# First block's query path and Exp table load inside the transform stage, its last stores by POOL, row scalings an item later, operand offsets of narrow matmuls

## The chip, the cores and the metric

One core of a Trainium2 chip runs one program. A core has TensorE (PE in the rows of the profile; its weight loads are PEld), VectorE (DVE), ScalarE (ACT), GpSimd (POOL) and SyncE (SP), each with its own queue of instructions that it takes in order, and 16 DMA engines that move data between the device's memory and the on-chip memories. DMAs are issued here by SP and POOL, and wait in the queue of the engine that issues them. The metric is the device time of one execution in microseconds, the median of several runs.

## The reference

One encoder layer for two sequences of 1024 tokens of width 1024, all in float32. A modulated RMSNorm feeds latent attention (4 heads) and a 2-D Fourier transform side by side; both are projected out together, and a SwiGLU feed-forward follows.

```python
h = rmsnorm(x, g_mix) * (1.0 + sc1) + sh1
z = h @ w_in
q_lat, kv_lat, k_pe, f_in = z[..., :o1], z[..., o1:o2], z[..., o2:o3], z[..., o3:]
y_mla = mla_group(q_lat, kv_lat, k_pe, g_q_lat, w_uq, g_kv_lat, w_ukv)
y_four = fourier_group(f_in, w_four)
mix = jnp.concatenate([y_mla, y_four], axis=-1) @ w_out
x = x + ga1 * mix
h2 = rmsnorm(x, g_ffn) * (1.0 + sc2) + sh2
ffn = (jax.nn.silu(h2 @ w_gate) * (h2 @ w_up)) @ w_down
return x + ga2 * ffn
# mla_group, for each query block of a sequence:
#   sc = (q_nope . k_nope + rope(q_pe) . rope(k_pe)) * scale; p = softmax(sc); o = p @ v
# fourier_group: real(fft2(f_in, axes=(sequence, group channel), norm='ortho')) @ w_four
```

The result is normalised once more and returned for both sequences.

## The kernel before

Every matrix product is made of three fp32r matmuls (`mm3`, lines 78 to 80): an operand is split into a high part, cast by ACT (line 62), and a low part, the difference, made by DVE (line 63), and high × high, low × high and high × low add up in one bank of PSUM. PE runs through the stages one after the other:

- **Input projection** (to about 238 us): x is normalised, transposed, and multiplied with the folded input weights; the narrowest products are 448 columns wide (`bank<-wz`).
- **Transform** (238 to 330 us): the DFT of each sequence (`dft`) leaves parts A, B and a Nyquist row `ny`. `fourier_out(s, j)` multiplies them with the folded weights `wm`, `wn`: for each pair (j, g) two banks `pa` (7 matmuls) and `pb` (6), 13 of 512 columns together. ACT copies `pa` to `ea`, DVE makes `ed` = `ea` − `pb` and `ea` + `pb` (lines 135 and 138), and line 735 stores both to `fo_d` in device memory, 256 KB each. `ed` is a ring of three buffers for each sign: a sum can be written when the store of three pairs ago has landed. For j = 0 there are 7 more matmuls (`pn`) for the Nyquist rows. Ahead of the second sequence's eight pairs, `stage3_loads` issues on SP the loads of what attention needs (`ql`, `wqr`, `rc`, `rs`, `lat`, `ckv`) and splits the query weights `wqr` into `wq_h` and `wq_l`.
- **Attention** (330 to about 790 us): 64 items (2 sequences × 4 blocks of 256 rows × 4 heads × 2 halves). For each block the rotary part of the queries is made by `rope_q` (6 matmuls of 256 columns into `gb`; DVE makes three products `qt`, lines 868 to 870, POOL adds them, ACT and DVE split the sum to `qsk`) and turned by `rope_flip` (4 transposes to `pqt`, an ACT copy to `qp`). `absorb_q` makes the rest of a head's queries, `qa` (6 matmuls, then a split). An item's scores are ten matmuls of 512 columns into `ps_s` (lines 904 to 908, two halves), DVE takes the maximum `mx` (913) and `nb` (914), ACT the exponential (916), DVE the reciprocal and the scaling of `p` (917, 918). `flip_p` transposes `p` an item later (930), `values` multiplies with `ckv`. In the first block of each sequence `wv_split` splits the output weights `wv`. Work of earlier blocks is spread over the items: `out_step` gives eight items an output projection, the norm of the new rows (`norm2`: ACT squares, POOL computes `rs_r` in six small steps, DVE scales `xn` at line 824) and the transposes of `xn`.
- **Feed-forward** (from about 799 us): Strassen-like sums on POOL and DVE, and long rows of 512-wide matmuls.

A scheduler orders each engine's queue from the order of the program, its data and its own estimate of when things are ready; `issue_after(x)` lets an instruction into the queue only behind x. A tile's place in on-chip memory follows from the order in which tiles are declared; `tag` and `bufs` make a ring of places that is reused. PSUM has eight banks of 512 columns: eight of one ring `bank` in the transform stage, four for `ps_s`, two for `gb` and two for transposes in attention.

Of the kernel before, what the change touches and what calls it, by code (L numbers as in the profile page):

```python
# [52 lines left out]
def hybrid_encoder_kernel(ctx: ExitStack, tc: tile.TileContext, a: dict):  # L53
# [110 lines left out]
    with ExitStack() as st:  # L164
# [13 lines left out]

        wuqT = w.tile([P, HEADS, QL], F32, tag="hh0", name="wuqT")
        wq = w.tile([P, 2, 768], F32, tag="hl0", name="wq")  # L180
        wz_h = w.tile([P, NC, DZ], F32R, name="wz_h")
# [396 lines left out]
    def load_seq(s, lp=None):  # L578
        lat = [(e if s == 0 else lp).tile([P, 2, N], F32R, tag=f"lat{s}{i}", name=f"lat{s}{i}") for i in range(2)]
        ckv = [e.tile([P, 8, KVL], F32R, tag=f"ckv{i}", name=f"ckv{i}", bufs=1) for i in range(2)]  # L580
        for i in range(2):
            nc.sync.dma_start(rd(lat[i]), lat_d[s][i][:, 2:4, :])
        for i in range(2):
            nc.sync.dma_start(rd(ckv[i]), ckv_d[s][i])
        S[s] = (lat, ckv)
# [6 lines left out]

    def stage3_loads():
        wq_h = e.tile([P, 2, 768], F32R, name="wq_h")
        wq_l = e.tile([P, 2, 768], F32R, name="wq_l")
        load_q(0, 0)
        for c in range(2):
            wqr = half("wqr")
            wqr2 = half("wqr2")
            nc.sync.dma_start(wqr, wq_d[:, c, 0:512])  # L600
            nc.sync.dma_start(wqr2[:, :256], wq_d[:, c, 512:768])
            split(wq_h[:, c, 512:768], wq_l[:, c, 512:768], wqr2[:, :256])
            split(wq_h[:, c, 0:512], wq_l[:, c, 0:512], wqr)
        rc = e.tile([P, 8, ROPE], F32, name="rc")
        nc.sync.dma_start(rc, a["ropec"])
        rs = e.tile([P, 8, ROPE], F32, name="rs")
        nc.sync.dma_start(rs, a["ropes"])
        load_seq(0)
        return wq_h, wq_l, rc, rs

    with ExitStack() as st:
# [11 lines left out]
        nyt = w.tile([P, NT], F32R, name="ny")  # L623
# [24 lines left out]
        def dft(s):  # L648
            z, od = zh.pop(s)
            A = [w.tile([P, 2, NT], F32R, tag=f"A{i}", name=f"A{i}", bufs=1) for i in range(2)]  # L650
            B = [w.tile([P, 2, 512], F32R, tag=f"B{i}", name=f"B{i}", bufs=1) for i in range(2)]
            for q in (0, 2, 1) if s == 0 else (0, 1):
# [12 lines left out]
                if q == 2:  # L665
                    ah = w.tile([NY2, NT], F32R, name="nyh")
                    al = w.tile([NY2, NT], F32, name="nyl")
                else:
                    ah, al = A[0][:, q, :], A[1][:, q, :]
# [41 lines left out]
        def fourier_out(s, ABn, j):  # L711
# [3 lines left out]
            for g in range(2):  # L715
# [11 lines left out]
                add(ed[1], ea, pb, nc.vector)  # L727
                if j == 0:
                    pn = bank2()
                    for q in range(2):  # L730
                        mm3(pn[:2, :], A[0][:, q, 512:514], A[1][:, q, 512:514], wm[0][:, q, gs], wm[1][:, q, gs], q == 0, False)
                    nc.tensor.matmul(pn[:2, :], ny[:, 512:514], wn[:, gs], start=False, stop=True)
                    nc.scalar.copy(ed[1][0:1, :], pn[0:1, :])
                for u in range(2):
                    nc.sync.dma_start(fo_d[s][rows(j, u), gs], ed[u])
# [34 lines left out]
        for s in range(2):  # L770
            for j in (1, 2, 3, 0):
                fourier_out(s, abn, j)
# [4 lines left out]
            if s == 0:  # L777
# [8 lines left out]
                wq_h, wq_l, rc, rs = stage3_loads()  # L786
    P2.close()
# [28 lines left out]
    def norm2(s, b, u, pool):  # L816
# [7 lines left out]
        here["n"] = sq, nc.vector.tensor_scalar(out=xn, in0=x2, scalar1=r[:, 0:1], scalar2=None, op0=ALU.mult).ins  # L824
        S["xn", s, b, u] = xn

# [14 lines left out]
    def out_step(s, b, i):  # L841
# [5 lines left out]
        if i in (1, 3):  # L847
            norm2(s, b, i // 2, tl)
# [3 lines left out]
    with ExitStack() as st:  # L852
# [3 lines left out]

        def rope_q(s, b, u):
            ql = S["q", s, b]
            ti = 2 * b + u
            us = slice(u * P, u * P + P)  # L860
            pq = gbank()
            for c in range(2):
                mm3(pq[:, :256], ql[0][:, c, us], ql[1][:, c, us], wq_h[:, c, 512:], wq_l[:, c, 512:], c == 0, c == 1)
            pv = pq[:, :256].rearrange("p (h r) -> p h r", h=HEADS)
            t1 = half("qt1").rearrange("p (k h r) -> p k h r", k=2, h=HEADS)
            cb = rc[:, ti : ti + 1, :].broadcast_to([P, HEADS, ROPE])
            sb = rs[:, ti : ti + 1, :].broadcast_to([P, HEADS, ROPE])
            nc.vector.tensor_tensor(out=t1[:, 0], in0=pv, in1=cb, op=ALU.mult)
            nc.vector.tensor_tensor(out=t1[:, 1, :, :32], in0=pv[:, :, 32:], in1=sb[:, :, :32], op=ALU.mult)
            nc.vector.tensor_tensor(out=t1[:, 1, :, 32:], in0=pv[:, :, :32], in1=sb[:, :, 32:], op=ALU.mult)  # L870
            here["p"] = nc.gpsimd.tensor_tensor(out=t1[:, 0], in0=t1[:, 0], in1=t1[:, 1], op=ALU.add).ins
            sk = w.tile([P, HEADS, P], F32R, tag="sk", name="qsk", bufs=2)
            nc.scalar.copy(sk[:, :, :64], t1[:, 0])
            nc.vector.tensor_tensor(out=sk[:, :, 64:], in0=t1[:, 0], in1=rd(sk[:, :, :64]), op=ALU.subtract)
            S["sk", s, b, u] = sk

        def rope_flip(s, b, u):
            sk = S.pop(("sk", s, b, u))
            pt = tbank("pqt", F32R)
            for h in range(HEADS):  # L880
                nc.tensor.transpose(pt[:, h, :], sk[:, h, :], identr)
            qp = w.tile([P, HEADS, P], F32R, tag="qp", name="qp", bufs=4)
            nc.scalar.copy(qp, rd(pt))
            S["qp", s, b, u] = qp

        def absorb_q(s, b, h):
            ql = S["q", s, b]
            pq = gbank()
            hs = slice(h * P, h * P + P)
            for c in range(2):  # L890
                mm3(pq[:, :256], wq_h[:, c, hs], wq_l[:, c, hs], ql[0][:, c, :], ql[1][:, c, :], c == 0, c == 1)
            qa = [w.tile([P, 256], F32R, tag=f"qa{i}", name=f"qa{i}", bufs=3) for i in range(2)]
            split(qa[0], qa[1], pq[:, :256])
            S["qa", s, b, h] = qa

        def scores(s, b, h, u):
# [17 lines left out]
            nc.vector.tensor_scalar(out=nb, in0=mx, scalar1=-SCALE, scalar2=None, op0=ALU.mult)  # L914
            p = w.tile([P, N], F32, tag="p", name="p", bufs=3)
            nc.scalar.activation(p, ps, AF.Exp, bias=nb, scale=SCALE, accum_out=sm)
# [27 lines left out]
        for u in range(2):  # L944
            rope_q(0, 0, u)
        absorb_q(0, 0, 0)
        for u in range(2):
            rope_flip(0, 0, u)
# [28 lines left out]
        def wv_split(i):  # L977
            h, g = i % 4, i // 4
            gs = slice(512 * g, 512 * g + 512)
            split(wv[0][:, h, gs], wv[1][:, h, gs], S.pop(("wv", h, g)))  # L980
# [17 lines left out]
        for k in range(nit + 4):  # L998
# [7 lines left out]
            if k < nit:  # L1006
                s, b, h, u = items[k]
                scores(s, b, h, u)
                nxt = items[k + 8 - k % 8] if k + 8 - k % 8 < nit else None
                i = k % 8  # L1010
                if nxt is not None:
                    if i == 0:
                        load_q(*nxt[:2])
                    if i == 3 and nxt[1] == 0:
                        load_seq(nxt[0], w)
                    if i in (3, 4):
                        rope_q(*nxt[:2], i - 3)
                    if i in (5, 6):
                        rope_flip(*nxt[:2], i - 5)
                if u == 1 and k + 1 < nit:  # L1020
                    absorb_q(*items[k + 1][:3])
# [610 lines left out]
```

## Time and profile before

| | us |
|---|---|
| three runs, median (lowest to highest) | 2095.7 (2093.01 to 2097.82) |
| the profiled execution | 2097.92 |
| its span, first to last instruction | 2096.1 |

The granted clock of PE over the span was 0.987. The page gives for each engine the busy time, its share of the span and the number of instructions. A row of the slices cuts the span into 40 parts of 52.4 us, and each digit is a busy share in tenths, for PEclk the granted clock:

```profile
PE   5899998999999999999999999999999999999998
DVE  2657756766676678687777777666855565567675
ACT  2666524455565546233333346453333333336441
POOL 1455202111312314797787720225545444420142
PEclk8999999999999999999999999999999999999999
```

In a row of the timeline stand the start and the duration in us, the engine, the line, the operation, what is written and what is read, and in brackets how long the engine stood idle before it and what ended that. Matmuls follow each other faster than one of them lasts, so their pace is read from starts, not from durations. A row that ends in x and a number stands for so many instructions in a stretch.

### The profile page before, as it was taken

The numbers are of one execution on the slowest core, as the hardware profiler recorded it, in microseconds if no ns is written. First come the engines' busy times: TensorE is split into PE (matmuls) and PEld (weight loads), VectorE is DVE, ScalarE is ACT, GpSimd is POOL, SyncE is SP. The second block draws the span as 40 slices with busy tenths as digits, with TensorE's granted clock in tenths as the row PEclk, the third lists the DMA queues.
The fourth block names the chain that finished last, engine by engine and source line by source line (L and its number), as shares of the span: only waits on it lengthen the run. The fifth ranks groups of instructions, "written<-read, shape, count | busy, mean of one in ns | idle before, by whom it ended". The sixth has DMA issues, their size and how long they took to land. (4 is left out here: it accounts for less than half of the span.)

```text
span 2096.1 us, 28784 instructions
## 1 busy us (share of the span) xinstructions
PE 2013.3 (96%) x10044; PEld 1669.9 (80%) x10044; DVE 1398.5 (67%) x2087; ACT 905.6 (43%) x1763; POOL 827.8 (39%) x1018
## 2 busy tenths in 40 slices
PE   5899998999999999999999999999999999999998
PEld 2788876888888887788888888877788888888876
DVE  2657756766676678687777777666855565567675
ACT  2666524455565546233333346453333333336441
POOL 1455202111312314797787720225545444420142
PEclk8999999999999999999999999999999999999999
DMA  9585766444454345556555578674423232248662
GB/s 367 190 251 196 233 229 221 94 98 100 137 133 130 122 174 206 188 196 209 166 188 190 176 249 271 223 239 153 150 87 115 101 115 102 86 167 282 229 224 98
DMA packets 184255, 371.30 MB, mean 177 GB/s; under 512 B 19053, under 2 KB 58605, under 8 KB 181037
## 3 DMA queue, kind: packets, MB, share of 16 engines
q1 hardware_dynamic: 166252, 314.00, 45.0%
q0 software_dynamic: 17856, 55.45, 8.9%
q8 instruction: 79, 1.29, 0.2%
q14 instruction: 68, 0.55, 0.1%
HBM read 257.38 MB, written 120.39 MB: 180 GB/s over the span
## 5 line engine op out<-in xcount | busy, mean ns | idle before, releaser
L78 PE MATMUL bank<-H,wh 128*128 128x512 f32 x1232 | 483.7, 393 | 10.2 <-ACT val L1312 5.4
L80 PE MATMUL bank<-H,wl 128*128 128x512 f32 x1232 | 482.7, 392 | 1.9 <-DVE wl L63 1.9
L79 PE MATMUL bank<-H,wh 128*128 128x512 f32 x1232 | 482.9, 392 | 0.0
L138 DVE TENSOR_TENSOR val<-bank,val 128x512 f32<-128x512 f32 x244 | 166.8, 689 | 192.6 <-PE bank L80 186.2
L78 PEld LDWEIGHTS bank<-H,wh 128*128 128x128 f32 x1232 | 233.0, 189 | 62.5 <-DVE val L138 6.8
L80 PEld LDWEIGHTS bank<-H,wl 128*128 128x128 f32 x1232 | 233.1, 189 | 51.4 <-DVE wl L63 2.7
L79 PEld LDWEIGHTS bank<-H,wh 128*128 128x128 f32 x1232 | 233.2, 189 | 48.6
L63 DVE TENSOR_TENSOR wl<-draw,wh 128x512 fp32r<-128x512 f32 x286 | 201.1, 736 | 89.4 <-ACT wh L62 87.9
L62 ACT CAST wh<-draw 128x512 fp32r<-128x512 f32 x286 | 169.0, 620 | 159.1 <-PE bank L79 87.0
L79 PE MATMUL bank<-wl,wh 128*128 128x512 f32 x572 | 224.0, 392 | 3.1 <-DVE wl L63 3.1
L78 PE MATMUL bank<-wh 128*128 128x512 f32 x572 | 222.9, 390 | 0.2 <-ACT wh L62 0.2
L80 PE MATMUL bank<-wh,wl 128*128 128x512 f32 x572 | 222.8, 389 | 0.0
L138 POOL TENSOR_TENSOR val<-val 128x512 f32<-128x512 f32 x58 | 82.5, 1429 | 350.6 <-DVE val L1413 186.8
L62 ACT CAST wh<-rgu 128x512 fp32r<-128x512 f32 x172 | 107.0, 623 | 261.1 <-PE bank L79 201.9
L62 ACT CAST wh<-val 128x512 fp32r<-128x512 f32 x133 | 82.2, 621 | 271.7 <-PE bank L79 245.7
L63 DVE TENSOR_TENSOR wl<-val,wh 128x512 fp32r<-128x512 f32 x133 | 128.4, 968 | 73.0 <-ACT wh L62 72.8
L135 POOL TENSOR_TENSOR val<-rgu 128x512 f32<-128x512 f32 x84 | 119.4, 1421 | 121.4 <-DMA rgu<-in_wgu_dram 86.4
L63 DVE TENSOR_TENSOR wl<-rgu,wh 128x512 fp32r<-128x512 f32 x172 | 158.3, 921 | 5.8 <-ACT wh L62 5.6
L79 PEld LDWEIGHTS bank<-wl,wh 128*128 128x128 f32 x572 | 107.4, 188 | 28.9 <-DVE wl L63 7.0
L78 PEld LDWEIGHTS bank<-wh 128*128 128x128 f32 x572 | 107.4, 188 | 23.1 <-ACT wh L62 0.6
L80 PEld LDWEIGHTS bank<-wh,wl 128*128 128x128 f32 x572 | 107.4, 188 | 21.8
L135 POOL TENSOR_TENSOR val<-val 128x512 f32<-128x512 f32 x89 | 119.2, 1358 | 1.3
(332 smaller groups left out, 4068.0 us busy)
## 6 DMA issues: line engine op xcount, KB each, us to landing
rgu<-in_wgu_dram SPq DMA_DIRECT2D x86, 512.0 KB
draw<-s_d SPq DMA_DIRECT2D x143, 256.0 KB
s_d<-val POOLq DMA_DIRECT2D x88, 256.0 KB, 4.0
draw<-t_d SPq DMA_DIRECT2D x88, 256.0 KB
s_d<-val SPq DMA_DIRECT2D x66, 256.0 KB
draw<-in_w_down_dram SPq DMA_DIRECT2D x55, 256.0 KB
wada<-in_w_ada_dram SPq DMA_DIRECT2D x13, 1024.0 KB
xt<-in_x_dram SPq DMA_DIRECT2D x16, 512.0 KB
```

The lines of the kernel that those rows point to most:

```text
L62: here["a"] = nc.scalar.copy(hi, src).ins
L63: here["v"] = nc.vector.tensor_tensor(out=lo, in0=src, in1=rd(hi), op=ALU.subtract).ins
L78: nc.tensor.matmul(out, lh, rh, start=first, stop=False, skip_group_check=cont)
L79: nc.tensor.matmul(out, lh, rl, start=False, stop=False, skip_group_check=cont)
L80: nc.tensor.matmul(out, ll, rh, start=False, stop=last, skip_group_check=cont)
L135: return eng.tensor_tensor(out=out, in0=x, in1=y, op=ALU.subtract).ins
L138: eng.tensor_tensor(out=out, in0=x, in1=y, op=ALU.add)
```

## The change

- **Query path of the first block.** `rope_q`, `rope_flip` and `absorb_q` move out of the attention stage and take their bank as an argument. Both `rope_q` and the first `absorb_q` now run ahead of the last two pairs (j = 0) of the second sequence's `fourier_out`; the two `rope_flip` run inside the first of these pairs.
- **Stores.** The 16 stores of the second sequence's `fourier_out` are issued by POOL, those of the first still by SP.
- **Loads.** `wqr` is loaded 768 wide into the places that `ckv` takes later, one load for each of two rows; the `ckv` loads then wait for the splits.
- **Tables.** A one-element Exp runs on ACT behind the last split of `stage3_loads`, and a one-element Silu behind the last item's exponential.
- **Splits of wv** are issued behind the `nb` and the exponential of an item.
- **Row scalings.** In `out_step`, `norm2` keeps the scaling of `xn` back; it is issued in the next item, behind that item's `nb`.
- **Offsets.** Tiles of 32 bytes a row that hold nothing (`phase_...`) shift the tiles behind them, and rows of 514 floats get places of 528.

PE at the end of the transform stage, before: the last pair's Nyquist matmuls, then the query path (absorb, rope) in attention's own banks.

```order
L79 MATMUL bank<-wm_3307,A_3208 2x512
L80 MATMUL bank<-wm_3306,A_3209 2x512
L732 MATMUL bank<-wn,ny 2x512
L78 MATMUL gb<-wq_h,ql_3380 128x256
L79 MATMUL gb<-wq_l,ql_3380 128x256
L80 MATMUL gb<-wq_h,ql_3381 128x256
```

And now, the end of the query path, and behind it the first of the last two pairs:

```order
L78 MATMUL bank<-ql_3383,wq_h 128x256
L79 MATMUL bank<-ql_3384,wq_h 128x256
L80 MATMUL bank<-ql_3383,wq_l 128x256
L78 MATMUL bank<-wm_3308,A_3210 128x512
L79 MATMUL bank<-wm_3309,A_3210 128x512
```

and the end of that pair, with the transposes of the rotary part:

```order
L79 MATMUL bank<-wm_3309,B_3212 128x512
L80 MATMUL bank<-wm_3308,B_3213 128x512
L617 MATMUL pqt<-identr,qsk 128x128 x8
L78 MATMUL bank<-wm_3308,A_3210 2x512
L79 MATMUL bank<-wm_3309,A_3210 2x512
```

The query path stands ahead of the last two pairs, its transposes between the first of them and its Nyquist matmuls; after the second pair the scores follow at once.

POOL at the same place, before:

```order
L702 MEMSET wnr 128x512 x4
L871 TENSOR_TENSOR qt_3639<-qt_3639 128x256
L871 TENSOR_TENSOR qt_3654<-qt_3654 128x256
L974 TENSOR_TENSOR wvr_3714<-wvr_3714,gah 128x512 x4
L871 TENSOR_TENSOR qt_3845<-qt_3845 128x256
```

and now:

```order
L745 MEMSET wnr 128x512 x4
L781 DMA fo_d_101<-ed 128x512 x12
L608 TENSOR_TENSOR qt_3563<-qt_3563 128x256
L608 TENSOR_TENSOR qt_3578<-qt_3578 128x256
L781 DMA fo_d_101<-ed 128x512 x4
L989 TENSOR_TENSOR wvr_3720<-wvr_3720,gah 128x512 x4
L608 TENSOR_TENSOR qt_3851<-qt_3851 128x256
```

The two rope additions (`qt`) stand behind twelve stores; the last four stores follow them.

DVE where a row scaling (`xn`) of the first sequence meets the next item's maximum (`mx`), before:

```order
L814 TENSOR_TENSOR x_4397<-x_4397,gb 128x512
L824 TENSOR_SCALAR xn<-x_4397,rs_r 128x1024
L913 TENSOR_REDUCE mx<-ps_s 128x1
L63 TENSOR_TENSOR qa_4742<-gb,qa_4741 128x256
L914 TENSOR_SCALAR nb<-mx 128x1
```

and now:

```order
L866 TENSOR_TENSOR x_4403<-x_4403,gb 128x512
L933 TENSOR_REDUCE mx<-ps_s 128x1
L934 TENSOR_SCALAR nb<-mx 128x1
L879 TENSOR_SCALAR xn<-x_4403,rs_r 128x1024
L63 TENSOR_TENSOR qa_4748<-gb,qa_4747 128x256
```

The scaling has gone behind the maximum and `nb`, and still stands ahead of the low half of `qa`.

The diff, cut to its core:

```diff
+        w.tile([P, 8], F32, name="phase_hh")
         wuqT = w.tile([P, HEADS, QL], F32, tag="hh0", name="wuqT")
         wq = w.tile([P, 2, 768], F32, tag="hl0", name="wq")
+        w.tile([P, 8], F32, name="phase_wz")
...
+    def rope_q(s, b, u, bankf):
...
+    def rope_flip(s, b, u, pt):
...
+    def absorb_q(s, b, h, bankf):
...
+        e.tile([P, 8], F32, name="phase_ql")
         load_q(0, 0)
+        e.tile([P, 8], F32, name="phase_hv")
+        hv = [half("hv") for _ in range(2)]
+        rc = e.tile([P, 8, ROPE], F32, name="rc")
+        rs = e.tile([P, 8, ROPE], F32, name="rs")
+        lat = [e.tile([P, 2, N], F32R, tag=f"lat0{i}", name=f"lat0{i}") for i in range(2)]
+        e.tile([P, 8], F32, name="phase_kv")
         for c in range(2):
-            wqr = half("wqr")
-            wqr2 = half("wqr2")
-            nc.sync.dma_start(wqr, wq_d[:, c, 0:512])
-            nc.sync.dma_start(wqr2[:, :256], wq_d[:, c, 512:768])
-            split(wq_h[:, c, 512:768], wq_l[:, c, 512:768], wqr2[:, :256])
-            split(wq_h[:, c, 0:512], wq_l[:, c, 0:512], wqr)
-        rc = e.tile([P, 8, ROPE], F32, name="rc")
+            wqr = e.tile([P, 768], F32, tag=f"ckv{c}", name="wqr", bufs=1)
+            nc.sync.dma_start(wqr, wq_d[:, c])
+            split(wq_h[:, c, 512:768], wq_l[:, c, 512:768], wqr[:, 512:768])
+            split(wq_h[:, c, 0:512], wq_l[:, c, 0:512], wqr[:, 0:512])
+        e.tile([P, 8], F32, name="phase_e")
         nc.sync.dma_start(rc, a["ropec"])
-        rs = e.tile([P, 8, ROPE], F32, name="rs")
         nc.sync.dma_start(rs, a["ropes"])
-        load_seq(0)
+        load_seq(0, lat)
...
-        nyt = w.tile([P, NT], F32R, name="ny")
+        nyt = w.tile([P, 528], F32R, name="ny")[:, :NT]
...
-            A = [w.tile([P, 2, NT], F32R, tag=f"A{i}", name=f"A{i}", bufs=1) for i in range(2)]
+            A = [w.tile([P, 2, 528], F32R, tag=f"A{i}", name=f"A{i}", bufs=1)[:, :, :NT] for i in range(2)]
...
+                if (s, j, g) == (1, 0, 0):
+                    for u in range(2):
+                        rope_flip(0, 0, u, pp.tile([P, 512], F32R, tag="b", name="pqt").rearrange("p (a b) -> p a b", a=4))
...
-                    nc.sync.dma_start(fo_d[s][rows(j, u), gs], ed[u])
+                    (nc.sync if s == 0 else nc.gpsimd).dma_start(fo_d[s][rows(j, u), gs], ed[u])
...
+                if s == 1 and j == 0:
+                    for u in range(2):
+                        rope_q(0, 0, u, bank2)
+                    absorb_q(0, 0, 0, bank2)
...
+                with tc.issue_after(here["a"]):
+                    nc.scalar.activation(tiny.tile([P, 1], F32, name="warm"), cmask[:, 0:1], AF.Exp)
...
-    def norm2(s, b, u, pool):
+    def norm2(s, b, u, pool, later=False):
...
-        here["n"] = sq, nc.vector.tensor_scalar(out=xn, in0=x2, scalar1=r[:, 0:1], scalar2=None, op0=ALU.mult).ins
         S["xn", s, b, u] = xn
+
+        def scale():
+            here["n"] = sq, nc.vector.tensor_scalar(out=xn, in0=x2, scalar1=r[:, 0:1], scalar2=None, op0=ALU.mult).ins
+
+        if later:
+            S["scale"] = scale
+        else:
+            scale()
...
-            norm2(s, b, i // 2, tl)
+            norm2(s, b, i // 2, tl, True)
...
-        for u in range(2):
-            rope_q(0, 0, u)
-        absorb_q(0, 0, 0)
-        for u in range(2):
-            rope_flip(0, 0, u)
...
-            split(wv[0][:, h, gs], wv[1][:, h, gs], S.pop(("wv", h, g)))
+            with tc.issue_after(here["nb"]), tc.issue_after(here["exp"]):
+                split(wv[0][:, h, gs], wv[1][:, h, gs], S.pop(("wv", h, g)))
...
+                if "scale" in S:
+                    with tc.issue_after(here["nb"]):
+                        S.pop("scale")()
+                if k == nit - 1:
+                    with tc.issue_after(here["exp"]):
+                        nc.scalar.activation(tiny.tile([P, 1], F32, name="warm"), cmask[:, 0:1], AF.Silu)
```

87 lines of the change are left out of this document (41 added, 46 removed).

## The prediction

> **What bounds the kernel now.** I read the page's busy shares first, then the slices, then windows around the slices in which TensorE (PE) is not full.
>
> ```profile
> PE 2013.3 (96%) x10044; PEld 1669.9 (80%) x10044; DVE 1398.5 (67%) x2087; ACT 905.6 (43%) x1763; POOL 827.8 (39%) x1018
> ```
>
> PE is busy 96% of 2096.1 us, so the change can only win where PE stands still or runs at a lower clock. The windows (span, then busy time of PE, PEld, DVE, ACT, POOL, then granted clock, DMA share, GB/s) show where that is near the change:
>
> ```profile
> 300.00:320.00 20.00, 20.00 (x91) 16.25 (x90) 10.21 (x27) 5.59 (x11) 0.22 (x1) 1.00 0.57 192
> 320.00:340.00 20.00, 16.76 (x79) 12.23 (x78) 9.37 (x19) 5.62 (x12) 1.46 (x2) 0.91 0.95 320
> 340.00:360.00 20.00, 15.59 (x72) 13.00 (x71) 14.92 (x25) 12.16 (x22) 12.69 (x9) 0.83 0.39 120
> 360.00:380.00 20.00, 19.53 (x132) 17.53 (x133) 17.72 (x37) 11.70 (x24) 2.30 (x3) 1.00 0.40 135
> ```
>
> The transform stage ends at 330 us and attention begins. In those 40 us PE is idle 3.24 + 4.41 = 7.65 us, and the clock is down by 0.09 and 0.17 of 20 us, which is 1.8 + 3.4 = 5.2 us; together 12.9 us, where the windows on both sides lose 0 and 0.5. Some of the low clock may fall into idle time, so 12.9 is what I take for the whole of it, not a floor.
>
> The timeline tells why (start, duration, work, and in brackets the idle time before it and what ended it):
>
> ```profile
> 326.01 0.40 PE L80 MATMUL bank<-wm,A 128*128 128x512 f32 x1
> 328.32 0.40 PE L80 MATMUL bank<-wm,B 128*128 128x512 f32 x1
> 328.32 0.69 DVE L135 TENSOR_TENSOR ed<-ea,bank 128x512 f32<-128x512 f32 x1 [6.96 <-DMA fo_d<-ed]
> ...
> 333.54 0.39 PE L78 MATMUL gb<-wq_h,ql 128*128 128x256 f32 x1 [3.20 <-DVE ed L138]
> ```
>
> First stall: VectorE (DVE) waited 6.96 us for a store of ed to land, then had eight sums in arrears, and PE, which needs the banks that they read, stood 3.2 us. The stores are late because SP issues them behind the attention loads:
>
> ```profile
> 311.04 0.43 SPq L582 DMA_DIRECT2D lat<-lat_d  x1
> 315.88 0.33 SPq L600 DMA_DIRECT2D wqr<-wq_d  x1
> 318.15 16.33 SPq L735 DMA_DIRECT2D fo_d<-ed  x14
> ```
>
> SP stood 4.4 us (311.47 to 315.88) in front of the second wqr load, and only then came 14 stores, over 16.33 us.
>
> ```profile
> 343.71 1.12 DVE L63 TENSOR_TENSOR wv<-wvr,wv 128x512 fp32r<-128x512 f32 x1 [1.30 <-ACT wv L62]
> 344.96 1.53 DVE L63 TENSOR_TENSOR wv<-wvr,wv 128x512 fp32r<-128x512 f32 x1
> 346.42 1.21 DVE L913 TENSOR_REDUCE mx<-ps_s 128x1 f32<-128x1024 f32 x1
> 346.62 1.28 ACT L916 ACT_TABLE_LOAD   x1
> 347.91 1.11 ACT L916 ACTIVATE p<-ps_s,nb 128x1024 f32<-128x1024 f32 x1
> 348.14 0.27 DVE L870 TENSOR_TENSOR qt<-gb,rs 128x128 f32<-128x128 f32 x1
> 348.56 0.55 PE L78 MATMUL gb<-ql,wq_h 128*128 128x256 f32 x1 [3.96 <-DVE qt L870]
> ```
>
> Second stall: the rope products (qt) of the next block free a bank that PE needs, but stand on DVE behind two splits of wv (2.65 us) and the second maximum; ScalarE (ACT) casts wv too, then loads the Exp table, before the first exponential.
>
> **The change part by part.** *Transition.* Three edits aim at these 12.9 us. The 16 stores of the second sequence go to POOL, so SP's loads no longer stand ahead of them. A POOL store is seen elsewhere in this kernel:
>
> ```profile
> L1248 POOL DMA_DIRECT2D s_d<-val x88: 539/557/653, 854.3 to 1883.1; - x88
> DMA to landing us min/median/max: 2.3/4.0/6.1
> ```
>
> It takes 0.56 us of POOL and lands in 4.0 us, 6.1 at most. PE makes a pair of banks in 13 matmuls; the two L80 rows are ten apart, 2.31 us, so 0.231 each and 3.0 us a pair. The ed ring is three deep, so a buffer has about 9 us less the 1.4 us of its two sums; two issues and the landing need 1.1 + 6.1 = 7.2. It holds, and POOL has 1.1 us of work in each 3.0. On POOL the two rope additions stand behind 12 stores; the last of those follows its own sum, which is before the rope products on DVE in any case.
>
> The first block's query path (12 + 6 matmuls of 256 columns) runs ahead of the last two bank pairs. Its long chain was bare:
>
> ```profile
> 334.55 0.42 DVE L868 TENSOR_TENSOR qt<-gb,rc 128x256 f32<-128x256 f32 x1 [1.07 <-PE gb L80]
> ...
> 337.92 0.41 DVE L874 TENSOR_TENSOR qsk<-qt,qsk 128x256 fp32r<-128x256 f32 x1
> ```
>
> From the first product to the second qsk it takes 338.33 − 334.55 = 3.8 us, at the low clock. In its new place PE has 6 matmuls of absorption (0.7 us) and 13 of 512 columns (3.0) before the eight transposes, 3.7 together: at most 0.4 us of waiting. Then 7 + 13 + 7 matmuls (27 × 0.231 = 6.2 us) cover the two qp copies.
>
> The table load (1.28 us) moves between copies of banks on ACT, which is busy 5.59 of 20 us there: no cost. The wv splits (1.12 and 1.53 us on DVE above) now come after an exponential, one an item, so qt and the maxima are no longer behind them. PE starts the first scores just after the last Fourier matmul; the first probabilities need from the end of item 0's scores a maximum (1.2), nb (0.15), exponential (1.1), and, by estimate from xn and nb, reciprocal and scaling (1.1), 3.6 us, plus handovers that I put at 1.0 by the gaps between the rows above: 4.6. PE has until then the scores of item 1 (10 × 0.231 = 2.3), 12 matmuls of 256 columns at half that (1.4) and half of item 2's scores (1.2): 4.9. So it is just even, and I leave 1.0 us of idle time. Without any cover that chain costs what the second stall cost. Transition: 12.9 − 1.0 = **11.9 us gained**; bounds 0 (stalls of the same size) and 12.9.
>
> *Row scalings an item later.* Before the change xn stands on DVE ahead of the maximum of the next item, and waits for the norm's scalar from POOL. The waits of PE between 400 and 790 us hold five such stalls (total, times, longest), and the timeline shows the first:
>
> ```profile
> PE ps_s L906 <- DVE nb L914: 7.4, 5, 2.1
> ```
>
> ```profile
> 437.00 0.76 DVE L824 TENSOR_SCALAR xn<-x,rs_r 128x1024 f32<-128x1024 f32 x1 [3.70 <-ACT ht L837]
> 437.67 1.22 DVE L913 TENSOR_REDUCE mx<-ps_s 128x1 f32<-128x1024 f32 x1
> 438.80 0.41 DVE L63 TENSOR_TENSOR qa<-gb,qa 128x256 fp32r<-128x256 f32 x1
> 439.27 0.50 PE L906 MATMUL ps_s<-lat,qa 128*128 128x512 f32 x1 [1.10 <-DVE nb L914]
> ```
>
> The matmul needs qa's low half, so DVE's order is the whole matter. The scores that mx reads are done here at 435.8 (the last one starts at 435.38), DVE idle:
>
> ```profile
> 435.38 0.39 PE L908 MATMUL ps_s<-lat,qp 128*128 128x512 f32 x1
> 663.27 1.75 DVE L824 TENSOR_SCALAR xn<-x,rs_r 128x1024 f32<-128x1024 f32 x1 [3.68 <-ACT ht L837]
> 666.53 0.50 PE L906 MATMUL ps_s<-lat,qa 128*128 128x512 f32 x1 [2.08 <-DVE nb L914]
> ```
>
> In the new order mx takes 435.8 to 437.0, nb 0.15, xn 437.15 to 437.9, qa to 438.35: PE goes on at 438.4 instead of 439.27, 0.9 us earlier. In the stalls of 2.08, where xn takes 1.75 beside a POOL sum, the same order gives 663.4 + 1.75 + 0.41 = 665.6 against 666.5, again 0.9. Five times 0.9 is **4.5 us gained**; bounds 0 (qa is still behind xn, and waits with it) and 7.4. xn itself is about 0.15 us later (437.15 for 437.00), which nothing behind it feels: its transposes come an item later.
>
> *Address offsets.* The small tiles and rows of 528 shift operands by 32 bytes. In the input projection the loop's blocks alternate between two pairs of offsets, in pairs, and so does the pace (first and last of 24 matmuls):
>
> ```profile
> 85.47 0.36 PE L78 MATMUL bank<-wz_h,hh 128*128 128x448 f32 x1
> 90.07 0.36 PE L80 MATMUL bank<-wz_h,hl 128*128 128x448 f32 x1
> 109.82 0.37 PE L78 MATMUL bank<-wz_h,hh 128*128 128x448 f32 x1
> 114.57 0.36 PE L80 MATMUL bank<-wz_h,hl 128*128 128x448 f32 x1
> ```
>
> 23 steps take 4.60 us where the offsets modulo 64 bytes are 32 and 0, and 4.75 where they are 32 and 32; all are 32 and 0 after the change. Half of the 384 matmuls, at 6.5 ns, would be 1.2 us; this stage also waits for its inputs, so I take 0.6. The 720 values matmuls of 256 columns (x240 for each of three lines) change in the same way:
>
> ```profile
> L78 PE MATMUL gb<-pt,ckv 128*128 128x256 f32 x240 | 69.3, 289 | 0.0
> ```
>
> At half the step (half the bytes moved) this could be 720 × 3 ns = 2.3 us, or nothing, as I see no pair of offsets of it in the trace; I take 0.4. **1.0 us gained**, bounds 0 and 3.5.
>
> *Silu table.* It moves from 812 us to the end of attention:
>
> ```profile
> 812.06 1.28 ACT L1321 ACT_TABLE_LOAD   x1
> 813.15 0.68 DVE L138 TENSOR_TENSOR val<-bank,val 128x512 f32<-128x512 f32 x1
> 813.88 0.50 PE L78 MATMUL bank<-H,wh 128*128 128x512 f32 x1 [1.18 <-DVE val L138]
> ```
>
> PE waits there for DVE's val, not for ACT, so this brings 0; bounds −0.3 and 0.5.
>
> Sum: 11.9 + 4.5 + 1.0 + 0 = 17.4 us. The profiled execution took 2097.9 us (span 2096.1 and 1.8 around it), so 2080.5 on its account; it lies 2.2 us above the median of 2095.7, so **2078.3 us** for a median.
>
> **The rivals.** *The first softmax stays bare (24%).* Scores of two items are all the work that PE has while DVE and ACT make the first probabilities; I found 4.9 us of matmuls against about 4.6. If the chain is 4 us longer, the 340 to 360 window keeps its loss, 4.41 + 3.4 = 7.8 us: 2078.3 + 7.8 − 1.0 = 2085. For it: the rows of 343 to 348 show three engines crowded there. Against it: table load and wv splits are gone from that chain.
> In this trace a stop of 3.2 us is followed by a low clock (0.91), and the one of 2.08 at 666 is not:
>
> ```profile
> 650.00:680.00 30.00, 27.59 (x176) 24.05 (x175) 18.70 (x32) 17.71 (x39) 7.66 (x11) 1.00 0.49 150
> ```
>
> The Trainium skill, TensorE: Matmul & The Clock Gate, section What's actually happening, has the clock halved after an idle window of about 3.4 us; the trace agrees as far as these two stops go, and by that rule a stop that stays shorter costs only itself: at 3.4 us for my 1.0, 2080.7.
>
> *The scalings gain nothing (10%).* qa stays behind xn, and PE waits as before: 2078.3 + 4.5 = 2083.
>
> *POOL's stores become the wait (slower, 8%).* If POOL could not have three or more stores in flight, each 4.0 us to land, 16 take 64 us where PE makes eight pairs in 24; ed would fill after three pairs, rope's additions would come behind the twelfth store, and PE would stop for up to 64 − 24 = 40 us instead of 12.9: 2095.7 + 40 − 12.9 − 5.5 + 5 (low clock) = 2122. It decides from a store pair slower than 3.0 us on, and exceeds the old time from 12.9 + 5.5 = 18.4 us of stops. Against it: the L1248 rows sit 0.56 us each and in pairs, with no wait for a landing. For it: DMA share is 0.95 at 320 to 340, where SP's stores took 16.33 / 14 = 1.17 us each to issue; at that pace POOL needs 2.3 us a pair, still under 3.0.
> The Trainium skill, SBUF — State Buffer, section Summary: rules for kernel authors, speaks against the move: descriptors that GpSimd writes are starved while DVE runs in a faster two-port mode, so use SP's or ACT's hardware queue. If every store waited for one DVE sum of 0.69 us it would take 1.25, 2.5 us a pair, which still fits; no run here shows it.
>
> *Nothing moves that decides (6%).* DMA share is 0.95 in the first window; if the loads fill it as before, POOL's stores land as late as SP's did, the ring is held as before, and of the 5.5 us elsewhere half comes: 2095.7 − 2.7 = 2093.
>
> **How the numbers follow.** My forecast has 52%, the rivals 24, 10, 8 and 6. A measurement of this kernel tells about 0.2% (4.2 us) from no change. The forecast and the first two rivals are faster by more, 0.86; nothing moves: same, 0.06; stores: slower, 0.08. Low end: transition 12.9, scalings 7.4, addresses 3.5, table 0.5, together 24.3 or 2071.4. High end: both smaller rivals together, 2085 + 4.5, about 2090, with 0.14 left above (the last two rivals) and a little below the low end. Range 2071 to 2090.
>
> **What would show it.** Right: DVE no longer waits for fo_d<-ed near 320 to 330; PE busy over 19 of 20 us and clock 1.00 in the two windows of the transition; L906 waits for nb under 1 us each; wz matmuls at 200 ns throughout. Wrong: PE idle before pqt (rope addition late), before the first ppt (softmax bare), or DVE waiting for POOL's stores. An unknown stall elsewhere in attention, from PE reaching work earlier than its loads, would break the sum.

## The result and the profile after

The changed kernel took 2095.3 us (median of 12 runs, 2092.94 to 2099.37), the kernel before 2094.19 us (12 runs, 2090.89 to 2097.82). The ratio is 1.0004 with a 95% interval of 0.9995 to 1.0013: no change. Forecast were 2078.3 us, and a range of 2071 to 2090.

The gain was there, and was given back elsewhere. The windows of the transition in the profile after (span, then busy time of PE, PEld, DVE, ACT, POOL, clock, DMA share, GB/s) show the first part of it:

```profile
300.00:320.00 20.00, 20.00 (x91) 16.32 (x90) 12.13 (x31) 7.76 (x14) 5.51 (x10) 1.00 0.89 327
320.00:340.00 20.00, 20.00 (x109) 15.33 (x108) 11.04 (x25) 6.71 (x13) 9.71 (x12) 1.00 0.75 272
340.00:360.00 20.00, 18.45 (x121) 16.06 (x120) 18.11 (x35) 12.39 (x25) 6.49 (x6) 1.00 0.13 42
```

PE is idle 1.55 us in 320 to 360 where it was 7.65, and the clock stays at 1.00. The timeline after shows the scores following the last Fourier matmul at once, and the first feed-forward matmul:

```profile
331.65 0.39 PE L778 MATMUL bank<-wn,ny 128*2 128x512 f32 x1
331.90 0.47 PE L924 MATMUL ps_s<-lat,qa 128*128 128x512 f32 x1
...
778.84 0.40 PE L78 MATMUL bank<-H,wh 128*128 128x512 f32 x1
```

In the profile before, that matmul stands here:

```profile
798.75 0.39 PE L78 MATMUL bank<-H,wh 128*128 128x512 f32 x1
```

So the changed kernel enters the feed-forward 19.9 us earlier. Then it loses. The same view of one undisturbed stretch of the feed-forward, first before and then after the change:

```profile
900.00:1150.00 250.00, 249.66 (x1100) 206.11 (x1099) 186.49 (x185) 78.27 (x131) 204.68 (x187) 1.00 0.56 188
```

```profile
900.00:1150.00 250.00, 250.00 (x1077) 202.98 (x1076) 178.21 (x180) 76.89 (x129) 199.18 (x181) 1.00 0.53 182
```

PE is busy throughout and at full clock in both, but starts 1077 matmuls in 250 us instead of 1100: one every 232.1 ns instead of every 227.3. A busy share can't show that; the count in brackets does. These are the matmuls of `H` with the up weights (`bank<-H,wh` and `bank<-H,wl`), 3 × 1232 = 3696 of them. Unrounded the step is 4.85 ns longer, and 3696 × 4.85 ns = 17.9 us. The down matmuls, whose two operands both lie in the places of `wh` and `wl`, keep their 227 ns. From the first to the last of the up matmuls of each sequence the traces show 431.3 us before and 438.8 after for the first sequence, 431.0 and 439.9 for the second; these stretches have waits in them too, and grow by 16.4 us together.

What differs for `H`? In the compiled program, its tiles lie 128 bytes higher than before (`H00` at 77408 instead of 77280), while the weights lie where they lay (151520). The diff doesn't name `H`. The 128 bytes are the two one-element warm-up results: their name `warm` is new in the pool of small tiles, which gives every name four places of 32 bytes, and `H` is laid out behind that pool. Before, the two operands were a multiple of 256 bytes apart; after, 128 more.

In the two traces the gain of 19.9 us and the loss of 16.4 leave 3.5 us, and the changed kernel's profiled execution is 3.8 us the shorter of the two (2094.11 us against 2097.92). It is no gain of the medians: the execution before was 3.7 us above its median of 12 runs, the one after 1.2 below, and −3.8 + 3.7 + 1.2 = +1.1, the distance of the medians.

### The profile page after: what moved, and what is told of

Read it like the earlier page. It is cut to its first block, busy times and chain, and to the rows that moved or that the text cites. A ratio compares the mean times of both kernels' runs of the same rounds, so it can differ in the third digit from the quotient of the medians.

```text
span 2092.3 us, 28786 instructions
## 1 busy us (share of the span) xinstructions
PE 2024.3 (97%) x10044; PEld 1665.8 (80%) x10044; DVE 1399.9 (67%) x2087; ACT 902.8 (43%) x1765; POOL 840.1 (40%) x1034
## 5 line engine op out<-in xcount | busy, mean ns | idle before, releaser
L78 PE MATMUL bank<-H,wh 128*128 128x512 f32 x1232 | 487.9, 396 | 11.9 <-DVE val L138 7.5
L138 POOL TENSOR_TENSOR val<-val 128x512 f32<-128x512 f32 x58 | 83.0, 1439 | 365.3 <-DVE val L1435 187.1
L63 DVE TENSOR_TENSOR wl<-val,wh 128x512 fp32r<-128x512 f32 x133 | 143.1, 1078 | 82.2 <-ACT wh L62 82.2
L933 DVE TENSOR_REDUCE mx<-ps_s 128x1 f32<-128x1024 f32 x64 | 78.2, 1222 | 62.1 <-PE ps_s L928 61.5
```

The lines of the kernel that those rows point to most:

```text
L63: here["v"] = nc.vector.tensor_tensor(out=lo, in0=src, in1=rd(hi), op=ALU.subtract).ins
L78: nc.tensor.matmul(out, lh, rh, start=first, stop=False, skip_group_check=cont)
L138: eng.tensor_tensor(out=out, in0=x, in1=y, op=ALU.add)
L933: nc.vector.tensor_reduce(out=mx, in_=ps, axis=AX.X, op=ALU.max)
```

## The experiments

My theory after the result: the place of `H` takes 15 to 18 us, and everything else in the change gains about 19. The rivals: PE is slower in the feed-forward for another reason (it stands less before; DMA or POOL run differently), or the slow pace only hides stalls that come back. Each run is compared with the kernel before on the same chip in the same batch, so two runs of different batches are best compared by their ratios. A (1) behind a time marks a single execution.

| run | median (runs) | before | ratio, 95% interval |
|---|---|---|---|
| e1_no_shift | 2077.33 (5) | 2096.88 | 0.9906, 0.9892 to 0.9919 |
| e2_before_128 | 2114.63 (4) | 2096.88 | 1.0081, 1.0065 to 1.0097 |
| e3_before_256 | 2097.89 (1) | 2096.88 | |
| e4_before_64 | 2100.87 (1) | 2096.88 | |
| e5_before_32 | 2118.72 (1) | 2094.95 | |
| e6_before_160 | 2119.55 (1) | 2094.95 | |
| e7_before_scale | 2085.34 (4) | 2094.90 | 0.9959, 0.9944 to 0.9974 |
| e8_sp_stores | 2080.56 (1) | 2094.90 | |
| e9_no_phase | 2075.95 (4) | 2094.90 | 0.9911, 0.9897 to 0.9924 |
| e10_scores_0 | 2078.27 (5) | 2094.90 | 0.9920, 0.9907 to 0.9933 |
| e11_path_back | 2083.98 (4) | 2096.11 | 0.9940, 0.9923 to 0.9956 |
| e12_wv_free | 2075.83 (4) | 2096.11 | 0.9905, 0.9890 to 0.9920 |

### The 128 bytes taken out

```diff
-                    nc.scalar.activation(tiny.tile([P, 1], F32, name="warm"), cmask[:, 0:1], AF.Exp)
+                    nc.scalar.activation(tiny.tile([P, 1], F32, name="pc"), cmask[:, 0:1], AF.Exp)
...
-                        nc.scalar.activation(tiny.tile([P, 1], F32, name="warm"), cmask[:, 0:1], AF.Silu)
+                        nc.scalar.activation(tiny.tile([P, 1], F32, name="pc"), cmask[:, 0:1], AF.Silu)
```

> The changed kernel with its two one-element warm-up results put into a ring that exists already (pc), so that no new place is taken in the pool of small tiles and the feed-forward's H tiles lie 128 bytes lower, where they lay before the change. Theory (place): the change gained 19.9 us up to the feed-forward and gave back 14.7 us there, because all 3696 matmuls of H with the up weights start every 231 to 232 ns instead of 227 when H is 128 bytes off against the weights. Then H matmuls are at 227 ns again and the time is 2095.3 - 14.7 = 2080.6 us (2077 to 2083). Rival 1 (PE is slower in the feed-forward because it stood less before, or through DMA traffic or POOL's work): still 232 ns, 2095. Rival 2 (the slower pace hides stalls that come back): 227 ns, but 2090 or more.

Measured: 2077.33 us, 19.6 us under the kernel before, 0.9906 (0.9892 to 0.9919). The stretch of the feed-forward in its profile:

```profile
900.00:1150.00 250.00, 249.81 (x1103) 206.52 (x1102) 189.14 (x184) 78.28 (x131) 205.75 (x186) 1.00 0.55 184
```

1103 matmuls, the old pace. The same instructions in the same order are faster by 18 us (by the medians; 20 by the ratios 1.0004 and 0.9906) when four places of 32 bytes go. Both rivals fall.

### The 128 bytes alone, and other distances

Unused tiles at the start of the pool of small tiles, in the kernel before; here four of 32 bytes, and 8, 2, 1 and 5 in the other runs:

```diff
     tiny = ctx.enter_context(tc.tile_pool(name="tiny", bufs=4))
+    tiny.tile([P, 8], F32, name="shift0", bufs=1)
+    tiny.tile([P, 8], F32, name="shift1", bufs=1)
+    tiny.tile([P, 8], F32, name="shift2", bufs=1)
+    tiny.tile([P, 8], F32, name="shift3", bufs=1)
```

> The kernel before, with 128 bytes a partition of unused tiles in the pool of small tiles and nothing else. Theory (place): H matmuls start every 231 to 232 ns, the feed-forward is 15 us longer, 2109 us (2106 to 2112). Rivals (anything that the change does in time: order, stalls, queues): 227 ns and 2094 us.

> The kernel before with 256 unused bytes. If the distance of the two operands counts modulo 256 bytes or less: 227 ns, 2094 us. If it counts modulo 512 or more, or any shift costs: 231 ns or more, 2109 us.

> The kernel before with 64 unused bytes. If only the offset modulo 64 bytes counts, as my prediction had it: 227 ns, 2094 us (but then the 128 bytes of the other kernel would not count either). If the distance modulo 128 or 256 bytes counts: slower than 227 ns, between 2096 and 2115 us.

> The kernel before with 32 unused bytes: the offset modulo 64 bytes of H against the weights becomes 32 to 0, the distance modulo 256 is 32. If the distance modulo 256 sets the pace in steps of 64: 227 to 229 ns. If unequal offsets modulo 64 are faster, as the input projection suggested: 225 ns or less. If they are slower than the 128 bytes of e2: over 233 ns.

> The kernel before with 160 unused bytes, distance 160 modulo 256, offsets modulo 64 unequal. By the distance alone, between 128 (232.6 ns) and 192: 229 to 233 ns, 2105 to 2114 us. By the input projection's 448-wide matmuls, which are fastest at 160 and slowest at 0: 227 ns or less.

The same stretch in the five profiles, in the order 128, 256, 64, 32 and 160 bytes:

```profile
900.00:1150.00 250.00, 250.00 (x1078) 202.67 (x1077) 178.16 (x181) 76.92 (x129) 202.15 (x183) 1.00 0.53 183
```

```profile
900.00:1150.00 250.00, 249.82 (x1103) 206.54 (x1102) 186.26 (x184) 78.10 (x131) 205.38 (x187) 1.00 0.56 190
```

```profile
900.00:1150.00 250.00, 249.82 (x1091) 204.34 (x1090) 186.69 (x182) 77.54 (x130) 203.48 (x186) 1.00 0.55 186
```

```profile
900.00:1150.00 250.00, 250.00 (x1073) 200.81 (x1072) 179.74 (x179) 76.43 (x128) 200.69 (x181) 1.00 0.53 185
```

```profile
900.00:1150.00 250.00, 250.00 (x1068) 200.97 (x1067) 178.38 (x178) 75.73 (x128) 198.69 (x180) 1.00 0.53 183
```

With 128 bytes the kernel before, which has no other part of the change, takes the changed kernel's pace, 250 / 1078 = 231.9 ns, and loses 17.8 us (13.6 to 20.3 by the interval); I had expected 15. The unused tiles move other operands too: half of the 640 score matmuls go from 229 to 233 ns, about 1 us of the loss. With 256 bytes the old pace is back (226.7), so a distance of 256 bytes is as good as none. In between: 64 bytes 229.1 ns, 32 bytes 233.0, 160 bytes 234.1. The guess that unequal offsets modulo 64 bytes might be faster for 512 columns is wrong: 32 and 160 are the two slowest of the five, 24 us slower in their one run each, and 160 is slower than both of my expectations for it.

One rival is left: that the place of `H` counts by itself, and not its distance from the other operand. The traces settle it. In the last 132 matmuls of the program (`bank<-H`) both operands lie in places of `H`, so unused tiles move them together and leave their distance alone. A third of them, first before, then with 160 bytes (the three numbers behind the count are recorded durations in ns, then come the first and the last start):

```profile
L78 PE MATMUL bank<-H x44: 388/389/390, 2056.6 to 2085.9; 128*128 128x512 f32 x44
```

```profile
L78 PE MATMUL bank<-H x44: 387/389/390, 2078.2 to 2107.5; 128*128 128x512 f32 x44
```

Both take 29.3 us for 129 steps, 227 ns a step, while the up matmuls of the same two runs take 227 and 234. So what counts here is the distance.

### The offsets that the change does name

e1 without the empty tiles and with rows of 514 again, so that all matmul operands lie as far apart as before:

```diff
-        w.tile([P, 8], F32, name="phase_hh")
...
-        e.tile([P, 8], F32, name="phase_ql")
...
-            A = [w.tile([P, 2, 528], F32R, tag=f"A{i}", name=f"A{i}", bufs=1)[:, :, :NT] for i in range(2)]
+            A = [w.tile([P, 2, NT], F32R, tag=f"A{i}", name=f"A{i}", bufs=1) for i in range(2)]
```

> The version of e1 without the small unused tiles and the rows of 528, so that all the operands of matmuls lie as far from each other as in the kernel before. Prediction's term: the offsets bring 1.0 us (0 to 3.5), so this is 2078.3. What e1's trace shows (matmuls of 256 columns 1 to 6 ns faster, scores of 512 columns 3 to 4 ns slower, 448 columns the same) makes 1152 x 2 to 3 ns gained against 640 x 3.7 lost: 0 within 1 us, 2077. If the offsets do what the change's words say: 2080 or more.

Measured: 2075.95 us, 0.9911 (0.9897 to 0.9924) against e1's 0.9906: no difference that can be told. The offsets bring nothing as a whole. Their parts can be seen in the starts of the matmuls: with them the 256-column matmuls of `pt` and `ckv` go from a median of 120 ns to 119 (117 in the changed kernel), and the scores, whose `qa` and `qp` have moved away from `lat`, from means of 229 to 233.

The next kernel tries to have both, and brings the scores' operands back to a multiple of 256 bytes:

```diff
-        e.tile([P, 8], F32, name="phase_e")
+        e.tile([P, 56], F32, name="phase_e")
...
-                        load_seq(nxt[0], [w.tile([P, 2, N], F32R, tag=f"lat1{i}", name=f"lat1{i}") for i in range(2)])
+                        load_seq(nxt[0], (w.tile([P, 48], F32, name="phase_lat1"), [w.tile([P, 2, N], F32R, tag=f"lat1{i}", name=f"lat1{i}") for i in range(2)])[1])
```

> The version of e1 with 192 bytes more ahead of qa and qp and 192 ahead of the second sequence's lat, so that the two operands of every score matmul lie a multiple of 256 bytes apart, as they did in the kernel before. If the distance modulo 256 bytes sets the pace: scores of 512 columns fall from 233 to 229 ns, 640 x 3.7 = 2.4 us, 2075 us. If not: 2077.3. Matmuls of pt and ckv come to a distance of 224, whose pace is not known.

The scores went from 233 to about 231 ns, not to 229, and the time, 2078.27 us (2073.7 to 2081.52), is not to be told from e1's. Half of the expected step at best; what else sets the scores' pace stays open.

### The row scalings alone

The kernel before with `norm2`'s scaling kept back to the next item, behind `nb`, and nothing else of the change:

```diff
-            norm2(s, b, i // 2, tl)
+            norm2(s, b, i // 2, tl, True)
...
+                if "scale" in S:
+                    with tc.issue_after(here["nb"]):
+                        S.pop("scale")()
```

> The kernel before with the row scalings an item later and nothing else of the change. Prediction's term: the five stalls of 7.4 us at the third score matmul shrink by 0.9 us each, 4.5 us in all, 2092 us against 2096.5 (attention's last seven blocks 4 to 5 us shorter in the trace). Rival (the low half of qa still waits behind the scaling): 0, stalls of 7 us as before. Rival (all of it goes, since the scaling no longer stands ahead of anything late): 7 us, and the trace shows no stall over 0.3 us there.

Measured: 0.9959 (0.9944 to 0.9974), 5.4 to 11.7 us faster. Attention after its first block is 7.9 us shorter in the trace. The waits of PE from 380 to 770 us (what waited and for what, total, times, longest; the line numbers are 7 higher than before):

```profile
PE ppt L937 <- DVE p L925: 2.0, 9, 0.6
PE ps_s L913 <- DVE qa L63: 1.0, 2, 0.5
```

Of 7.4 us 1.0 is left, nearer to the second rival than to my 4.5. The timeline shows why:

```profile
433.72 0.76 DVE L827 TENSOR_SCALAR xn<-x,rs_r 128x1024 f32<-128x1024 f32 x1
...
434.35 0.39 PE L912 MATMUL ps_s<-lat,qa 128*128 128x512 f32 x1
434.39 0.42 DVE L63 TENSOR_TENSOR qa<-gb,qa 128x256 fp32r<-128x256 f32 x1
434.58 0.28 PE L79 MATMUL gb<-pt,ckv 128*128 128x256 f32 x1
434.69 0.28 PE L80 MATMUL gb<-pt,ckv 128*128 128x256 f32 x1
434.81 0.28 PE L78 MATMUL gb<-pt,ckv 128*128 128x256 f32 x1
434.93 0.28 PE L79 MATMUL gb<-pt,ckv 128*128 128x256 f32 x1
435.05 0.40 PE L913 MATMUL ps_s<-lat,qa 128*128 128x512 f32 x1
```

`qa` still stands behind `xn`, as I had it, and is ready at 434.81. But the scheduler has moved four `values` matmuls, 0.47 us, ahead of the score matmul that waits for it, and PE does not stop.

### What carries the transition

Three runs undo one part each in e1. First the stores, back on SP:

```diff
-                    (nc.sync if s == 0 else nc.gpsimd).dma_start(fo_d[s][rows(j, u), gs], ed[u])
+                    nc.sync.dma_start(fo_d[s][rows(j, u), gs], ed[u])
```

> The version of e1 with the 16 stores of the second sequence issued by SP again, the rest as in e1. If the stores on POOL carry the first half of the transition's gain: VectorE waits some 5 us or more for a store in 315 to 335 us, PE stands 2 to 4 us before the scores and the clock falls; the first scores start at 336 to 340 us instead of 332.6, and the time is 5 to 8 us above e1, 2082 to 2085. If the query path and its earlier loads carry it alone: first scores at 332.6 within 0.5, 2077.

Its stores and the loads behind them on SP, and its waits of DVE for stores from 310 to 335 us:

```profile
317.81 15.10 SPq L781 DMA_DIRECT2D fo_d<-ed  x14
332.96 0.98 SPq L591 DMA_DIRECT2D ql<-lat_d  x2
334.04 0.41 SPq L968 DMA_DIRECT2D gah<-ga_d  x1
334.56 3.72 SPq L988 DMA_DIRECT2D wvr<-wo_d  x7
```

```profile
DVE ed L135 <- DMA fo_d<-ed: 0.7, 1, 0.7
```

Neither expectation held whole. The stores are as late as before the change, but DVE waits for them 0.7 us only, and the scores start at 332.1, as the second has it, though the time is 3 us above it; I suppose that the query path ahead of the last two pairs, with its 18 matmuls, gives the ring its time, but that was not tried. What is lost, 3.3 us, is lost in block 0, whose last `values` matmul comes 58.2 us after its first score instead of 54.9; there SP's loads of `ql` and `wvr` stand behind the stores. That those loads are the way from the one to the other is read from the queue and was not tried. One run, 2080.56 us.

Then the query path, back at the start of attention:

```diff
-                if s == 1 and j == 0:
-                    for u in range(2):
-                        rope_q(0, 0, u, bank2)
-                    absorb_q(0, 0, 0, bank2)
...
+        for u in range(2):
+            rope_q(0, 0, u, gbank)
+        absorb_q(0, 0, 0, gbank)
+        for u in range(2):
+            rope_flip(0, 0, u, tbank("pqt", F32R))
```

> The version of e1 with the first block's query path back at the start of attention; stores by POOL, early loads, table load, wv splits and scalings as in e1. In e1 the first scores start 0.5 us after the last Fourier matmul and block 0 takes 54.9 us. If the query path's place hides its chain: scores start about 5 us after the last Fourier matmul (18 matmuls of 256 columns, 2.1 us, which leave the stage before, and 3 us of bare chain), time 2 to 4 us above e1, 2079 to 2082, and the clock stays at 1.00 if the stop is under 3 us. If the stores and early loads carry the transition alone: within 1 us of e1.

```profile
320.00:340.00 20.00, 18.90 (x98) 13.83 (x96) 9.30 (x18) 6.00 (x12) 10.02 (x12) 1.00 0.78 283
340.00:360.00 20.00, 17.18 (x98) 14.39 (x97) 16.97 (x35) 10.59 (x21) 6.88 (x6) 0.91 0.12 34
```

2083.98 us, 0.9940 (0.9923 to 0.9956): 12.1 us of gain are left of e1's 19.6, and in the trace the first feed-forward matmul comes 4.8 us later. That is more than I expected (2 to 4 us), and the costliest of the three parts to lose. PE is idle 3.92 us in the two windows, and against what I wrote the clock falls (0.91).

Last, the Exp table at the first exponential and the splits of wv free again:

```diff
-                with tc.issue_after(here["a"]):
-                    nc.scalar.activation(tiny.tile([P, 1], F32, name="pc"), cmask[:, 0:1], AF.Exp)
...
-            with tc.issue_after(here["nb"]), tc.issue_after(here["exp"]):
-                split(wv[0][:, h, gs], wv[1][:, h, gs], S.pop(("wv", h, g)))
+            split(wv[0][:, h, gs], wv[1][:, h, gs], S.pop(("wv", h, g)))
```

> The version of e1 with the Exp table loaded at the first exponential and the wv splits free to stand anywhere, as in the kernel before; the query path and the stores as in e1. If these two made the second stall (prediction): PE is idle 3 to 5 us in 335 to 360, with or without a low clock, block 0 takes 58 to 63 us in place of 54.9, time 2081 to 2085. If they do not matter once the query path is early: 54.9 within 0.7, 2077.

```profile
320.00:340.00 20.00, 18.66 (x100) 14.12 (x99) 10.64 (x23) 8.04 (x15) 9.92 (x13) 1.00 0.78 281
340.00:360.00 20.00, 18.32 (x117) 16.12 (x118) 18.74 (x38) 13.97 (x29) 7.66 (x6) 1.00 0.26 93
```

2075.83 us, 0.9905 (0.9890 to 0.9920), as e1. PE is idle 3.02 us in the two windows instead of e1's 1.6, the clock stays up, and block 0 takes 55.7 us for 54.9. With the query path early, the table load and the splits are worth a microsecond at most by the trace, which the times can't show.

So e1, e9, e10 and e12 all beat the kernel before, by about 0.8 to 0.95%, and with it the changed kernel, whose ratio is 1.0004. Which of them is best can't be told from these runs.

## Why the prediction was wrong, step by step

- **What bounds the kernel: right.** PE does, and time comes from where it stands or runs slower. The step was incomplete: PE's pace was read from idle time and clock alone, and a third thing, the start-to-start time at full clock, was looked at for the narrow matmuls only.
- **Transition, 11.9 us: right in size.** Idle time of the two windows fell from 7.65 to 1.55 us and the loss of clock from 5.2 to 0, which is 11.3; to the end of block 0 the trace gains 12.5. The shares were partly wrong. I put the first stall down to the stores and the second to the splits of wv and the table load. The runs show the query path as the largest part (7 us by the times, 5 by the traces), POOL's stores worth some 3 us by one run, and not at the place I named, and splits and table load about 1 or less. The stores did not land in the 4.0 us, 6.1 at most, that I took from elsewhere in the kernel. For the 16 that POOL issues the trace after has

```profile
DMA to landing us min/median/max: 2.3/6.4/8.4
```

  and with 8.4 + 1.1 us for the two issues the ring of three does not hold as I worked it out: DVE still waits 1.2 us for one store. PE did not stop for it.
- **Row scalings, 4.5 us: right in kind, too small.** Alone they bring 5.4 to 11.7 us. I moved DVE's order and kept PE's; PE's queue is ordered anew too, and covers the wait that is left.
- **Address offsets, 1.0 us gained, bounds 0 and 3.5: this step failed.** "The small tiles and rows of 528 shift operands by 32 bytes" was taken as the whole of it. The warm-up tiles shift one operand, `H`, of 3696 matmuls by 128 bytes; the step has no such term, and its bounds had no loss. It cost 16 to 18 us: 17.9 by the matmul counts, 16.4 by the stretches of the traces; e2, which moves more than `H`, lost 17.8. I looked at addresses modulo 64 bytes, by which `H` is unchanged. The trace before held a warning: the matmuls of `wm` and `A`, 512 wide like those of `H`, started every 231 ns (326.01 to 328.32 in ten steps), while those of the feed-forward kept 227, and I used the 231 without asking why. (In the compiled program the two operands there lie 64 to 128 bytes apart, modulo 256.) The gain that I did put down did not come either: e9, without the offsets, is as fast as e1. And 720 × 3 ns is 2.2 us, not 2.3, which changes nothing.
- **The input projection's pace: measured right, explained wrong.** 200 against 206.5 ns was put down to offsets of 32 and 0 against 32 and 32 modulo 64. After the change all of them are at 32 and 0, and the blocks still differ, as two blocks of the profile after show (first and last of 24):

```profile
109.81 0.36 PE L78 MATMUL bank<-wz_h,hh 128*128 128x448 f32 x1
114.51 0.36 PE L80 MATMUL bank<-wz_h,hl 128*128 128x448 f32 x1
...
131.68 0.37 PE L78 MATMUL bank<-wz_h,hh 128*128 128x448 f32 x1
136.29 0.36 PE L80 MATMUL bank<-wz_h,hl 128*128 128x448 f32 x1
```

  4.70 us for 23 steps (204 ns) where the distance modulo 256 is 32, 4.61 (200 ns) where it is 160; before it was 0 and 160. The 0.6 us that I took from it did not come.
- **Silu table, 0:** neither borne out nor refuted, since no run has this load alone. For the Exp load, which I also put at no cost, e12 finds no difference that can be told.
- **The rivals.** PE's wait at the first softmax is there, 1.5 us and not 4; POOL's stores did not become the wait. None of the rivals was the one that came, and the one on the slower side was sought in the queues, not in the layout. That 2093 us of the last rival lies nearest to the measured time is an accident: it had no gain in the transition and half of the gains elsewhere, while both the transition and the scalings gained more than forecast. The prediction's reading that a stop of PE shorter than about 3.4 us costs only itself agreed with two stops of one trace, and does not hold in the others (last section).

With the 128 bytes taken out, the forecast gain of 17.4 us stands beside 19.6 measured (17.0 to 22.6 by the interval). That is too little for the scalings and 1 us too much for the offsets, so that the sum fits is in part luck.

## What to carry to other kernels

A new tile moves every tile behind it: after each edit of pools, compare the addresses of the operands of the largest group of matmuls before and after, however far from the edit that group lies. Compare not only busy shares and idle time but the number of matmuls in an equal stretch where PE is full: 2% of pace on 3696 matmuls took back nearly all that the change had gained from stalls. When a change aims at several stalls and the total does not move, time the start of each stage first; here a single row, the first feed-forward matmul 19.9 us earlier, showed that the gain was real and where to look for the loss.

## What the runs showed of the hardware

- The pace of the 512-column fp32r matmuls of `H` depends on the distance in bytes, modulo 256, between the places of their two operands in on-chip memory, at full clock and with nothing waited for: 226.7 ns at 0 and 256 bytes, 229.1 at 64, 231.9 at 128, 233.0 at 32, 234.1 at 160. At 448 columns the order is another: 200 ns at 160, 204 to 206.5 at 0 and 32. No cause for it was tested, and e10's scores, 231 ns at a distance of 0, show that it is not the whole.
- The granted clock fell in e11, although no single wait of PE there was over 2 us. Its three longest kinds of waits from 320 to 390 us, and two rows of its slow stretch, 0.43 us apart for 512 columns, about twice the usual step:

```profile
PE ps_s L917 <- ACT qa L62: 1.8, 1, 1.8
PE pqt L617 <- DVE qsk L611: 0.8, 2, 0.4
PE ppt L943 <- DVE nb L927: 0.6, 1, 0.6
```

```profile
354.65 0.63 PE L920 MATMUL ps_s<-lat,qp 128*128 128x512 f32 x1
355.08 0.63 PE L921 MATMUL ps_s<-lat,qp 128*128 128x512 f32 x1
```

- The length of a stop does not tell whether the clock falls after it. In the kernel before, a single stop of 2.08 us at 666 us had no effect. The same stop before the same matmul in e2, and the 3.40 us behind it at a granted clock of 0.50:

```profile
666.14 0.50 PE L910 MATMUL ps_s<-lat,qa 128*128 128x512 f32 x1 [2.08 <-DVE nb L918]
667.00:670.40 3.40, 3.40 (x13) 2.94 (x12) 2.94 (x4) 0.39 (x2) 1.96 (x2) 0.50 0.79 223
```

  In e3 to e6 the clock from 650 to 680 us is 0.94, as in e2, and 1.00 in the kernel before. The other way round, the changed kernel has a stop of 3.06 us before 1440.2 us and a clock of 1.00 from 1430 to 1460 us. What decides was not tested.
